# Gated MLP: up projections with tokens on partitions, brought to channels by VectorE and DRAM

## Chip, core and metric

The kernel runs on one core of a Trainium2 chip. The metric is the device time of one execution in microseconds (us), as the median of several runs. A core has TensorE (PE, matrix products into PSUM), VectorE (DVE), ScalarE (ACT), GpSimd (POOL) and SyncE (SP), each with a queue of its own that it works through in order, and 16 DMA engines. PEld is the loading of weights into TensorE. SP's queue issues nearly all DMA transfers.

## What is computed

Two layers of an encoder on 256 tokens of 1024 channels, float32. Each layer has a token mixer (pooling and attention branches) and a gated MLP with a convolution of width 3 over the tokens. The change is in the MLP:

```python
def _conv_ffn(xn, w_up, conv_w, conv_b, w_down):      # xn: 256 x 1024
    a, gval = jnp.split(xn @ w_up, 2, axis=-1)         # w_up: 1024 x 5632
    a = depthwise_conv(a, conv_w, width 3, over tokens) + conv_b
    return (jax.nn.gelu(a) * gval) @ w_down            # w_down: 2816 x 1024
...
h = h + _conv_ffn(_rmsnorm(h, norm2[layer]), ...)
```

## The kernel before

**Numbers.** Float32 products are made of parts: every operand is split into a high part in a shorter format (fp32r) and the rest, and three products (high-high, high-low, low-high) are summed in PSUM. Tokens are in two halves t = 0, 1 (even and odd tokens), 128 each.

**Weights.** The class `Weights` (lines 95 to 223) loads all weights in 1 MB transfers into three buffers `raw` (line 134, on SP's queue) and splits each into two pieces of 128 x 1024: ACT casts the high part `wh` (line 197) and DVE subtracts to get the rest `wl` (line 198). Five pairs of split buffers exist; `W.get` (line 216) asks for pieces three ahead of the one in use. `loads_behind` and `queue_behind` keep named instructions ahead of a load or a split on their queue. The order of the loads and pieces is written out by hand in lines 257 to 299. `cols` takes 256 columns of a weight over all 1024 rows (rows of 1 KB), `rows` takes some rows with 512 or 1024 columns (rows of 2 or 4 KB).

**Order.** A scheduler orders each engine's instructions at build time from the order of the program and from when it thinks that buffers and data are there. On the chip, each engine then keeps that order.

**Two forms of a projection.** In the *channel form* (`proj`, line 528, `two_sums`, line 507) the weight piece is loaded into TensorE and the activations stream past it: 8 matmuls of 512 columns and 8 of 256 give 128 channels on partitions by 256 tokens. `add_up` (line 554) adds the two sums (an ACT copy out of PSUM, then a DVE addition). In the *token form* (`v_sum`, line 638, `by_tokens`, line 649) the activations are loaded into TensorE and 512 columns of the weight stream past: four pieces of 12 matmuls give two PSUM tiles of 128 tokens by 512 channels. `by_tokens` calls `then` after each piece.

**The MLP** has 22 groups of 128 channels (`NF`), f = 0 to 21. The convolution runs over tokens and so needs channels on partitions, and so does the down projection. The first four groups' `a` branch (`ENTRY = 4`) is made in the token form by `begin_mlp` (line 1179) while the norm is still under way, copied out of PSUM (`keep_entry`), transposed on TensorE (`turn_entry`, line 1210, tile `a_turn`) and copied to `a_first`. All other projections are in the channel form. `up(f)` (line 1230) then makes one group: ACT scales (line 1239), two DVE operations add the neighbours (lines 1240, 1243), a tanh form of gelu follows (lines 1252 to 1259), the gate is multiplied in (line 1260), and the product is split into the high part `actq` (line 1265) and the rest `actk` (line 1266). The loop in lines 1284 to 1289 makes two groups and then two steps of the down projection, which runs six groups behind (`LAG = 6`). The down projection is `residual_mm` (line 566): one piece of `w_down`, 12 matmuls into four PSUM tiles, for each group. It holds its last four groups back, so that the four output tiles end one after the other.

**The way through DRAM.** The attention stage has a transposition that the change uses again, `start_turn` (line 1014): DVE transposes blocks of 32 x 32 (line 1019), one transfer writes 512 KB to DRAM (line 1021), and four read it back with the blocks in their places (line 1027). SP issues all five.

Of the kernel before, what the change touches and what calls it, by code (L numbers as in the profile page):

```python
# [10 lines left out]
F32 = mybir.dt.float32  # L11
# [24 lines left out]

WARM = ((P,) * 6, (P // 2,), (P, P // 2))
PAIRS = (2, 4, 0, 1, 3, 5)
LAG = 6
ENTRY = 4  # L40
HALVES = (slice(0, 512), slice(512, D))
SEGMENTS = (HALVES, (slice(0, 512), slice(512, 768), slice(768, D)))

# [183 lines left out]
def encoder(ctx, tc, x, w_in, w_pool, pool_scale, w_a, w_b, w_o, norm1, norm2, w_up, conv_w,  # L227
# [13 lines left out]
    def cols(w, c0):  # L241

        src = w[:, c0 : c0 + 256].rearrange("(k p) c -> p k c", p=P)
        return W.add(
            src, (8, 256), [((lambda t, j=j: t[:, :, j * P : (j + 1) * P]), (8, P)) for j in (0, 1)]
        )

    def rows(w, r0, n=2, c0=0, width=1024, tag=None, pieces=2):

        src = w[r0 : r0 + n * P, c0 : c0 + width].rearrange("(k p) c -> p k c", p=P)  # L250
        h = n // pieces
        return W.add(
            src, (n, width), [((lambda t, j=j: t[:, j * h : (j + 1) * h, :]), (h, width)) for j in range(pieces)],
            tag,
        )

    first_up = []
    for l in range(DEPTH):
        for g in range(NG):
            c0 = C_V + g * 512  # L260
            slots = (("m2", 0, 2), ("m2", 1, 2), ("ybig",), ("at2",)) if g == 0 else ()
            for j in range(2):
                tag = "k1" if l == 0 and g == 1 and j == 0 else None
                W.use(rows(w_in[l], j * 512, 4, c0, 512, tag), slots[2 * j : 2 * j + 2])
        if l == 0:
            W.n_scaled = len(W.pieces)
        for c in range(3, -1, -1):
            W.use(cols(w_in[l], c * 256))
        for n, c in enumerate(PAIRS):
            pool = ([], [])  # L270
            if n == 1:
                pool = W.add(
                    w_pool[l].rearrange("g (k p) c -> p (g k) c", p=P), (8, 256),
                    [((lambda t, j=j: t[:, 4 * j : 4 * j + 4, :]), (4, 256)) for j in range(2)],
                )
                pool = (pool[:1], pool[1:])
            W.use(pool[0] + cols(w_in[l], C_Q + c * 256))
            W.use(pool[1] + cols(w_in[l], C_K + c * 256))
        for w, c0 in ((w_a[l], 0), (w_in[l], C_GP)):
            for c in (c0, c0 + 512):  # L280
                W.use(rows(w, 0, 4, c, 512) + rows(w, 512, 4, c, 512))
        for c in (0, 512):
            W.use(rows(w_in[l], 0, 4, C_GA + c, 512) + rows(w_in[l], 512, 4, C_GA + c, 512))
            W.use(rows(w_b[l], 0, 4, c, 512))
        for c in range(4):
            W.use(rows(w_o[l], c * 256))
        first_up.append((len(W.pieces), len(W.loads)))
        slots = (("v1",), ("ybig",), ("at2",))
        for j in range(2):
            tag = None if j else "k1"  # L290
            W.use(rows(w_up[l], j * 512, 4, 0, 512, tag), slots[2 * j : 2 * j + 2])
        for f in range(0, NF, 2):
            a = cols(w_up[l], f * P) if f >= ENTRY else []
            g = cols(w_up[l], DFF + f * P)
            W.use([a[0], g[0], a[1], g[1]] if a else g)
            if f >= LAG:
                W.use(rows(w_down[l], (f - LAG) * P))
        for f in range(NF - LAG, NF, 2):
            W.use(rows(w_down[l], f * P))


# [248 lines left out]
    def in_order(a):  # L550

        return a.rearrange("p (m t) -> p t m", t=2)

    def add_up(out, sums):

        nc.scalar.copy(out=out, in_=sums[1])
        nc.vector.tensor_add(out=out, in0=sums[0], in1=out)  # L557
# [77 lines left out]
    def v_tile():  # L635
        return acc.tile([P, 512], F32, tag="acc", name="v_ps")
# [26 lines left out]
    def to_chunks(rows, y, z, parts):  # L663
# [12 lines left out]
        made = nc.scalar.copy(out=hi, in_=z), nc.vector.tensor_sub(out=lo, in0=z, in1=hi.bitcast(F32))  # L676
        return turned, there, made

    def two_parts(tag, name):


        return big.tile([P, KD, 2, 2, P], F32R, tag=tag, name=name)
# [174 lines left out]
    for l in range(DEPTH):  # L857
# [154 lines left out]
        turned_p = big.tile([P, 2, 2 * 4, 4, 32], F32, tag="ybig", name="turned_p")  # L1012

        def start_turn(hh):


            y = sm.tile([P, 2, 4, 4, 32], F32, tag="gain", bufs=1, name="turning")
            for t in range(2):
                nc.vector.transpose(out=y[:, t].rearrange("p q c j -> p c q j"), in_=probs[hh, t])
            d = dram.tile([2 * P, 4, P], F32, tag="turning", bufs=2, name="turning")  # L1020
            nc.sync.dma_start(
                out=d.rearrange("(t p) q x -> p t (q x)", t=2),
                in_=y.rearrange("p t q c j -> p t (q c j)"),
            )
            z = turned_p[:, hh % 2]
            for q in range(4):
                there = nc.sync.dma_start(
                    out=z[32 * q : 32 * q + 32].rearrange("p a c j -> p a (c j)"),
                    in_=d[:, q].rearrange("(a i) x -> i a x", i=32),
                )  # L1030

            W.loads_behind[W.n_loaded + 1] = there
            if hh == HPG - 1:
                W.loads_behind[first_up[l][1]] = there

# [164 lines left out]
        acts = {}  # L1200


        a_first = big.tile([P, ENTRY, S], F32, tag="gates", name="a_first")

        def keep_entry(ps):
            r = sm.tile([P, ENTRY * P], F32, tag="p", bufs=3, name="a_rows")
            nc.scalar.copy(out=r, in_=ps)
            return r

        def turn_entry(t, r):  # L1210
            pt = mmp.tile([P, ENTRY, P], F32, tag="mm", name="a_turn")
            for f in range(ENTRY):
                nc.tensor.transpose(pt[:, f, :], r[:, f * P : (f + 1) * P], ident)
            av = a_first.rearrange("p f (m t) -> p f m t", t=2)[:, :, :, t]
            nc.vector.tensor_copy(av, pt)

        held, ps = entry
        first = keep_entry(ps)
        ps = v_tile()
        for n in range(4):  # L1220
            v_sum(ps, x2, 1, n, held[n])
            if n == 1:
                turn_entry(0, first)
        for i, _ in held:
            W.free(i)
        last = keep_entry(ps)
        g_first = [proj(x2)]
        turn_entry(1, last)

        def up(f):  # L1230
            w0, w1, w2, b = (prm[:, l, j * NF + f : j * NF + f + 1] for j in range(4))
            if f < ENTRY:
                a = a_first[:, f, :]
            else:
                a = sm.tile([P, S], F32, tag="u", name="a")
                add_up(in_order(a), [halves(b) for b in proj(x2, 1 + (f < NF - 4))])
            sums = g_first.pop() if f == 0 else proj(x2)
            y = sm.tile([P, S], F32, tag="s", name="y")
            nc.scalar.activation(y, a, AF.Identity, bias=b, scale=w1)  # L1239
            nc.vector.scalar_tensor_tensor(  # L1240
                out=y[:, 1:], in0=a[:, : S - 1], scalar=w0, in1=y[:, 1:], op0=ALU.mult, op1=ALU.add
            )
            nc.vector.scalar_tensor_tensor(  # L1243
                out=y[:, : S - 1], in0=a[:, 1:], scalar=w2, in1=y[:, : S - 1],
                op0=ALU.mult, op1=ALU.add,
            )
            g = sm.tile([P, 2, P], F32, tag="p", bufs=3, name="g")
            add_up(g, [halves(a) for a in sums])

            c = float(np.sqrt(2.0 / np.pi))  # L1250
            y2 = sm.tile([P, S], F32, tag="us", name="y2")
            nc.scalar.activation(y2, y, AF.Square, scale=float(np.sqrt(0.044715)))  # L1252
            nc.vector.scalar_tensor_tensor(
                out=y2, in0=y2, scalar=1.0, in1=y, op0=ALU.add, op1=ALU.mult
            )
            nc.scalar.activation(y2, y2, AF.Tanh, scale=c)
            nc.vector.scalar_tensor_tensor(
                out=y2, in0=y2, scalar=1.0, in1=y, op0=ALU.add, op1=ALU.mult
            )
            nc.vector.scalar_tensor_tensor(  # L1260
                out=g, in0=in_order(y2), scalar=0.5, in1=g, op0=ALU.mult, op1=ALU.mult
            )
            n = f % NH
            ah, al = (x[n >= HPG][:, n - HPG * (n >= HPG)] for x in (acth, actl))
            nc.scalar.copy(out=ah, in_=g)
            nc.vector.tensor_sub(out=al, in0=g, in1=ah.bitcast(F32))
            acts[f] = (ah, al)

        late = {}
        begun = []  # L1270
# [10 lines left out]
            lambda k: acts[k], NF, lambda *a: late["norm"].add(*a),  # L1281
            fill=begin_values if l + 1 < DEPTH else None, whole=(l + 1 == DEPTH),
        )
        for f in range(0, NF, 2):
            up(f)
            up(f + 1)
            if f >= LAG:
                next(down)
                next(down)
        if l + 1 < DEPTH:  # L1290
            x2 = two_parts("x", "x2")
            late["norm"] = Norm(to_channels(x2, mmp, g1))
# [33 lines left out]
```

## Time and profile before

| what | value |
|---|---|
| median of 3 runs | 864.71 us (864.32 to 864.93) |
| profiled execution | 864.36 us, span 862.6 us, granted clock 0.998 |
| busy PE, PEld | 855.9, 738.2 us |
| busy DVE, ACT, POOL | 665.2, 506.6, 32.6 us |
| DMA | 174.23 MB, mean 202 GB/s |
| TensorE in the down projection | 3 groups x184, 69.9 us each |
| weight splitting in all | DVE 331.6 us, ACT 285.4 us |

The busy time of an engine is what its instructions cover; the span runs from the first to the last instruction. A group row names line, engine, operation, written and read tile with shapes and count, then busy time and mean ns of one, then the idle time just before and who ended it. In the timeline, the first two numbers are start and duration in us.

### The profile page before, as it was taken

Reading aid. Unit: us, or ns where it says so; the run is one execution under the profiler, and the core shown is the slowest. Engines: PE = TensorE matmul, PEld = TensorE weight load, DVE = VectorE, ACT = ScalarE, POOL = GpSimd, SP = SyncE. Lnnn points to the kernel's source line nnn. Section 1 sums busy time; section 2 is a strip of 40 time slices with the busy share of each in tenths; the row PEclk is TensorE's granted clock in tenths of the full one; section 3 lists DMA queues with packets and bytes.
Section 4 is the critical chain, followed back from the end, with each engine's and each line's share of the span. In section 5 each row is a group of like instructions: output and inputs, shape, how many; then the busy total and the mean of one; then the engine's idle time right before and its main releaser. Section 6 shows DMA issues by size and latency. Waiting matters only on the chain.

```text
span 862.6 us, 12111 instructions
## 1 busy us (share of the span) xinstructions
PE 855.9 (99%) x4519; PEld 738.2 (86%) x4519; DVE 665.2 (77%) x1070; ACT 506.6 (59%) x831; POOL 32.6 (4%) x98
## 2 busy tenths in 40 slices
PE   9999999999999999999999999999999999999997
PEld 8888888888888888888888888988888888888886
DVE  7998796667769978888855987873776798887874
ACT  7756654455457766666545675543654586666662
POOL 1800000000010000000000000000000000000001
PEclk9999999999999999999999999999999999999999
DMA  9685556766745565565626565648767446556541
GB/s 335 210 253 198 195 169 222 243 229 226 261 164 195 183 211 192 169 229 191 241 98 210 180 202 188 207 171 257 244 236 277 164 150 221 173 189 205 193 147 49
DMA packets 130306, 174.23 MB, mean 202 GB/s; under 512 B 4600, under 2 KB 95424, under 8 KB 130248
## 3 DMA queue, kind: packets, MB, share of 16 engines
q1 hardware_dynamic: 130088, 173.20, 59.6%
q8 instruction: 35, 0.57, 0.3%
q10 hardware_dynamic: 160, 0.27, 0.1%
q14 instruction: 23, 0.19, 0.1%
HBM read 166.09 MB, written 7.36 MB: 201 GB/s over the span
## 4 chain that ended last, share of the span: by engine, by line
PE 99%; DVE 0%; ACT 0%; issue 0%; POOL 0%; POOLq 0%; ACTq 0%
PE proj_ps L520 46%; PE t_ps L644 18%; PE v_ps L644 6%; PE res_ps L562 6%; PE res_ps L563 6%; PE res_ps L564 6%; PE v_ps L849 3%; PE v_ps L756 1%; PE pool_ps L520 1%; PE o_ps L1056 1%; PE s_ps L988 1%; PE s_ps L983 1%; PE o_ps L1052 1%; PE xt_ps L458 1%; PE gain_ps L349 0%; PE xt_ps L704 0%
## 5 line engine op out<-in xcount | busy, mean ns | idle before, releaser
L198 DVE TENSOR_TENSOR wl<-raw,wh 128x1024 fp32r<-128x1024 f32 x274 | 331.6, 1220 | 97.9 <-ACT wh L197 62.2
L197 ACT CAST wh<-raw 128x1024 fp32r<-128x1024 f32 x274 | 285.4, 1050 | 109.4 <-PE t_ps L644 31.6
L520 PE MATMUL proj_ps<-x,wh 128*128 128x512 f32 x1152 | 273.5, 390 | 0.0
L520 PEld LDWEIGHTS proj_ps<-x,wh 128*128 128x128 f32 x1152 | 213.3, 188 | 42.5
L520 PEld LDWEIGHTS proj_ps<-x,wl 128*128 128x128 f32 x1152 | 145.0, 191 | 3.6
L520 PE MATMUL proj_ps<-x,wl 128*128 128x256 f32 x1152 | 147.9, 283 | 0.0
L644 PE MATMUL t_ps<-wh,x 128*128 128x512 f32 x256 | 79.9, 391 | 0.0
L562 PE MATMUL res_ps<-wh,actq 128*128 128x512 f32 (+1 forms) x184 | 69.9, 380 | 0.0
L564 PE MATMUL res_ps<-wh,actk 128*128 128x512 f32 (+1 forms) x184 | 69.9, 380 | 0.0
L563 PE MATMUL res_ps<-wl,actq 128*128 128x512 f32 (+1 forms) x184 | 69.9, 380 | 0.0
L644 PEld LDWEIGHTS t_ps<-wh,x 128*128 128x128 f32 x256 | 47.8, 188 | 9.8
L644 PE MATMUL t_ps<-wl,x 128*128 128x512 f32 x128 | 49.8, 389 | 0.0
L644 PE MATMUL t_ps<-wh,po 128*128 128x512 f32 x128 | 41.4, 395 | 0.0
L563 PEld LDWEIGHTS res_ps<-wl,actq 128*128 128x128 f32 x184 | 34.6, 188 | 6.6
L562 PEld LDWEIGHTS res_ps<-wh,actq 128*128 128x128 f32 x184 | 34.6, 188 | 6.6
L564 PEld LDWEIGHTS res_ps<-wh,actk 128*128 128x128 f32 x184 | 34.6, 188 | 6.6
L1252 ACT ACTIVATE y<-y 128x256 f32<-128x256 f32 x44 | 18.1, 416 | 28.4 <-DVE y L1243 28.3
L431 POOL TENSOR_SCALAR ss<-ss 128x1 f32<-128x1 f32 x8 | 2.2, 275 | 783.2 <-ACT junk L424 783.2
L1239 ACT ACTIVATE y<-a,prm 128x256 f32<-128x256 f32 x36 | 21.6, 600 | 14.7 <-DVE a L557 14.7
L644 PEld LDWEIGHTS t_ps<-wl,x 128*128 128x128 f32 x128 | 24.0, 188 | 5.0
L644 PEld LDWEIGHTS t_ps<-wh,po 128*128 128x128 f32 x128 | 24.0, 188 | 4.9
L424 ACT ACTIVATE junk<-h 128x512 f32<-128x512 f32 (+1 forms) x19 | 10.5, 554 | 29.0 <-DVE h L422 28.8
(206 smaller groups left out, 1170.3 us busy)
## 6 DMA issues: line engine op xcount, KB each, us to landing
raw<-in_w_in_dram SPq DMA_DIRECT2D x58, 1024.0 KB, 5.1
raw<-in_w_up_dram SPq DMA_DIRECT2D x44, 1024.0 KB, 7.1
raw<-in_w_down_dram SPq DMA_DIRECT2D x22, 1024.0 KB, 4.8
raw<-in_w_a_dram SPq DMA_DIRECT2D x8, 1024.0 KB
raw<-in_w_o_dram SPq DMA_DIRECT2D x8, 1024.0 KB
turning<-turning SPq DMA_DIRECT2D x8, 512.0 KB, 3.1
turned_p<-turning SPq DMA_DIRECT2D x32, 128.0 KB, 3.6
raw<-in_w_b_dram SPq DMA_DIRECT2D x4, 1024.0 KB, 4.9
```

The lines of the kernel that those rows point to most:

```text
L197: lambda: nc.scalar.copy(out=h, in_=src),
L198: lambda: nc.vector.tensor_sub(out=l, in0=src, in1=h.bitcast(F32)),
L424: nc.scalar.activation(junk[:, 0 : cc.stop - cc.start], h[:, t, cc], AF.Square, scale=D**-0.5, accum_out=ss[:, n : n + 1],)
L458: nc.tensor.transpose(pt[:, k, :], xn[:, c0 : c0 + P], ident)
L520: nc.tensor.matmul(out, w(k), x, start=(steps is first and k == 0), stop=(steps is last and k == nk - 1), skip_group_check=turns["rest"],)
L562: nc.tensor.matmul(ps, ah, wh, start=first, stop=False, skip_group_check=on)
L563: nc.tensor.matmul(ps, ah, wl, start=False, stop=False, skip_group_check=on)
L564: nc.tensor.matmul(ps, al, wh, start=False, stop=last, skip_group_check=on)
L644: nc.tensor.matmul(ps, x2[:, 2 * n + j, part, t, :], w[:, j, :], start=(n + m == 0), stop=(n == last and m == 5),)
L849: nc.tensor.matmul(ps[t], a[:, k, t, :], w[:, j, :], start=(k + m == 0), stop=(k == KD - 1 and m == 2),)
L1239: nc.scalar.activation(y, a, AF.Identity, bias=b, scale=w1)
L1252: nc.scalar.activation(y2, y, AF.Square, scale=float(np.sqrt(0.044715)))
```

## The change

Both up projections use the token form for f = 0 to 19, in five groups of 512 columns (`NQ = 5`); the channel form stays for f = 20 and 21. Each result (two PSUM tiles of 128 tokens by 512 channels) is brought to channels by `cross`, which is the body of `start_turn` made a function: two DVE transposes of 32 x 32 blocks out of PSUM, a write to DRAM, four reads into `za` (two buffers, `a` branch) or `zg` (one buffer, gate). `activate` (copy out of `za`, convolution, gelu into `soft`) and `times` (`soft` with the gate from `zg`, then the split) take the place of `up`. `then` puts them after the pieces of the next group's projections, with one step of the down projection after each piece of an `a` chunk from the third on. The order in a group n = 2, 3, 4 is: four pieces of `a` with four down steps between, then four pieces of `g`. The transposes on TensorE (`turn_entry`) go. Weights of the up projections are loaded by 512 columns and four blocks of rows, and the loads wait on SP's queue behind the crossing (`loads_behind` in `cross`).

```diff
-LAG = 6
-ENTRY = 4
+NQ = NF // 4
...
-        for f in range(0, NF, 2):
-            a = cols(w_up[l], f * P) if f >= ENTRY else []
-            g = cols(w_up[l], DFF + f * P)
-            W.use([a[0], g[0], a[1], g[1]] if a else g)
-            if f >= LAG:
-                W.use(rows(w_down[l], (f - LAG) * P))
-        for f in range(NF - LAG, NF, 2):
+        def four_up(c0, down=None):
+            for j in range(2):
+                up = rows(w_up[l], j * 512, 4, c0, 512)
+                if down is None:
+                    W.use(up)
+                else:
+                    d = rows(w_down[l], (down + 2 * j) * P)
+                    W.use([up[0], d[0], up[1], d[1]])
+        four_up(DFF)
+        for n in range(1, NQ):
+            four_up(n * 512, 4 * (n - 2) if n > 1 else None)
+            four_up(DFF + n * 512)
+        a, g = cols(w_up[l], 4 * NQ * P), cols(w_up[l], DFF + 4 * NQ * P)
+        for j in range(2):
+            W.use([a[j], g[j]] + rows(w_down[l], (4 * (NQ - 2) + 2 * j) * P))
+        for f in range(4 * (NQ - 1), NF, 2):
             W.use(rows(w_down[l], f * P))
...
+    def cross(rows, y, z, name, but=1):
+        for t in range(2):
+            nc.vector.transpose(out=y[:, t].rearrange("p q c j -> p c q j"), in_=rows[t])
+        d = dram.tile([2 * P, 4, P], F32, tag=name, bufs=2, name=name)
+        nc.sync.dma_start(
+            out=d.rearrange("(t p) q x -> p t (q x)", t=2),
+            in_=y.rearrange("p t q c j -> p t (q c j)"),
+        )
+        for q in range(4):
+            there = nc.sync.dma_start(
+                out=z[32 * q : 32 * q + 32].rearrange("p a c j -> p a (c j)"),
+                in_=d[:, q].rearrange("(a i) x -> i a x", i=32),
+            )
+        W.loads_behind[W.n_loaded + but] = there
+        return there
...
-            if n == 1:
-                turn_entry(0, first)
...
-        last = keep_entry(ps)
-        g_first = [proj(x2)]
-        turn_entry(1, last)
+        to_z((ps0, ps1), za[:, 0])
+        to_z(by_tokens(x2, 4), zg)
...
+        def activate(f):
+            n, i = divmod(f, 4)
+            a = sm.tile([P, S], F32, tag="u", name="a")
+            nc.scalar.copy(
+                out=a.rearrange("p (a j t) -> p t a j", t=2, j=32), in_=of_chunk(za[:, n % 2], i)
+            )
+            soften(convolved(f, a), soft[:, i])
+
+        def times(f):
+            g = sm.tile([P, 2, P], F32, tag="p", bufs=3, name="g")
+            nc.vector.scalar_tensor_tensor(
+                out=g.rearrange("p t (a j) -> p t a j", j=32),
+                in0=soft[:, f % 4].rearrange("p (a j t) -> p t a j", t=2, j=32), scalar=0.5,
+                in1=of_chunk(zg, f % 4), op0=ALU.mult, op1=ALU.mult,
+            )
+            keep_act(f, g)
...
-        for f in range(0, NF, 2):
-            up(f)
-            up(f + 1)
-            if f >= LAG:
-                next(down)
-                next(down)
+        def then(n, branch):
+            pieces = iter(range(4))
+            def work():
+                i = next(pieces)
+                f = 4 * (n - 1)
+                if branch:
+                    if i < 2:
+                        times(f + 2 + i)
+                else:
+                    if n > 1:
+                        next(down)
+                    activate(f + i)
+                    if i > 1:
+                        times(f + i - 2)
+            return work
+        for n in range(1, NQ):
+            to_z(by_tokens(x2, 4, then=then(n, 0)), za[:, n % 2])
+            to_z(by_tokens(x2, 4, then=then(n, 1)), zg)
+        f = 4 * (NQ - 1)
+        for j in range(2):
+            sums = proj(x2, 2), proj(x2)
+            next(down)
+            activate(f + 2 * j)
+            next(down)
+            activate(f + 2 * j + 1)
+            for i in range(2):
+                times(f + 2 * j + i)
+            up(*sums, 4 * NQ + j)
```

## The prediction

> **What bounds the kernel now.** I read the page's busy table and its chain first.
>
> ```profile
> PE 855.9 (99%) x4519; PEld 738.2 (86%) x4519; DVE 665.2 (77%) x1070; ACT 506.6 (59%) x831; POOL 32.6 (4%) x98
> PE 99%; DVE 0%; ACT 0%; issue 0%; POOL 0%; POOLq 0%; ACTq 0%
> ```
>
> TensorE (PE) is busy and is the chain throughout: a stop of it adds to the time one for one, and only work taken from it can shorten the time. Next, whether PE streams the new form faster. Two pieces of the chain in order of time (start us, us):
>
> ```profile
> 144.52 2.77 PE t_ps L644 x12
> 299.18 11.11 PE proj_ps L520 x64
> ```
>
> One weight piece multiplied with tokens on partitions is 12 matmuls and 2.77 us. The channel form takes 11.11 us for four projections, 2.78 each. So the change gives PE nothing for each projection. Then the MLP stage, by windows (us; busy and count of PE, PEld, DVE, ACT, POOL; granted clock, DMA share, GB/s):
>
> ```profile
> 264.00:297.00 33.00, 33.00 (x185) 28.89 (x185) 32.85 (x69) 26.14 (x54) 0.00 (x0) 1.00 0.50 174
> 330.00:363.00 33.00, 33.00 (x178) 28.59 (x177) 26.31 (x45) 21.11 (x37) 0.00 (x0) 1.00 0.58 192
> ```
>
> VectorE (DVE) is full at the MLP's start and has some 7 us free in each 33 us later, ScalarE (ACT) 12, the DMA engines 40%. PE never waits here, so this slack is what the change may use up. The durations, from the groups kept apart by form and from the timeline (start us, us):
>
> ```profile
> L198 DVE TENSOR_TENSOR wl<-raw,wh 128x1024 fp32r<-128x1024 f32 x274 | 331.6, 1220 | 97.9 <-ACT wh L197 62.2 <-PE proj_ps L520 33.7
> L197 ACT CAST wh<-raw 128x1024 fp32r<-128x1024 f32 x274 | 285.4, 1050 | 109.4 <-PE t_ps L644 31.6 <-PE res_ps L564 29.3 <-PE proj_ps L520 24.1
> L1019 DVE STREAM_TRANSPOSE turning<-p 128x512 f32<-128x512 f32 x16 | 10.8, 697 | 0.1
> 254.52 3.90 ACT L197 CAST wh<-raw 128x1024 fp32r<-128x1024 f32 x4
> 258.50 2.35 DVE L198 TENSOR_TENSOR wl<-raw,wh 128x1024 fp32r<-128x1024 f32 x2
> 270.96 0.75 DVE L1260 SCALAR_TENSOR_TENSOR g<-y,g 128x256 f32<-128x256 f32 x2
> 271.74 0.70 ACT L1265 CAST actq<-g 128x256 fp32r<-128x256 f32 x2
> 256.57 0.60 PE L1213 MATMUL a_turn<-ident,a_rows 128*128 128x128 f32 x4
> ```
>
> One is longer than the step to the next: a weight subtraction takes 1.22 us but a pair 2.35 (step 1.13), casts step 0.95, 256-wide operations on DVE 0.33 and on ACT 0.30.
>
> **The change, part by part.** *Taken from PE:* four groups of four `a_turn` transposes; the next matmuls start 0.36 us after a group does, so **-1.4 us**.
>
> *DVE and ACT totals, each layer.* 36 `add_up` pairs go (DVE 0.42, ACT about 0.38: -15.1 and -13.7), as do the `a_first` and `a_rows` copies (-1.4, -1.2). 10 crossings bring 20 transposes at 0.70 (+14.0 on DVE), and 20 copies out of `za` some 0.39 each on ACT (+7.8). DVE gets 2.5 us lighter, ACT 7. A transpose out of PSUM is not in the trace: I take the 0.70 of the row from SBUF, as `add_up` from PSUM (0.42) costs what 256-wide operations from SBUF do. At most I'd let it double (+0.7 where it counts), at least 0.5. None of this is on PE's path by its total.
>
> *DMA.* 20 crossings write 512 KB and read 4 x 128 KB: 21 MB on 174 MB. The rows `turning` (3.1 us to landing) and `turned_p` (3.6), with four issues of 0.44, give about 9 us a crossing. It is wanted more than 11 us after its source, so alone it costs nothing. All of it stands on SP's queue, where weight loads are behind it (a rival below). The `a` and `g` loads now have 2 KB rows, like those of `w_in` (5.1 us to landing, against 7.1 for `w_up` in 1 KB rows).
>
> *What is moved: the order on ACT and DVE.* Each works through its queue in the built order, so I followed the changed program's order with these durations. The steady groups n = 2, 3, 4 go like this. Near the end of an `a` chunk DVE has, in this order, the transpose of t=0, the transpose of t=1, the four products of `times` and their four subtractions, and **only then** the subtraction for the first weight piece of the following `g` chunk. ACT has that piece's cast behind the four copies of `keep_act`. The transpose waits for PE's last matmul of the chunk, so DVE and ACT stand idle ahead of it though the piece's raw data could be there. Let that matmul end at 0. The t=1 transpose starts at 0.05, products from 0.65 (0.33 each; the fourth waits for the first subtraction to free its tile, 2.7), its ACT copy 3.1, the weight cast 3.45 to 4.5, the weight subtraction 4.55 to 5.75. PE has one piece of the down projection (2.77) as cover and can run two matmuls (0.46) from the cast alone. It loses 5.8 - 2.77 - 0.46 = 2.6 us. Three groups, two layers: **+15.4 us**. At n = 1 the four pieces of the `g` chunk stand ahead of the transposes, so nothing is lost.
>
> The second place is the start of the first interleaved `a` chunk (n = 1), with no down piece as cover. DVE has the transposes of the `g` chunk, then the convolution of f = 0, 1 (four 255-wide operations; a dependent one starts 0.52 after its source, others 0.4: to 2.5), then two more, then the weight subtraction. ACT has two squares first, the second from 2.65, then the cast 2.95 to 4.0. Subtraction 4.05 to 5.3; minus 0.46 gives 4.85, twice: **+9.7 us**. The raw data of that weight come behind the first crossing on SP's queue (0.4 issue, 3.1 write, 1.8 for four issues, 0.4 and 5.1 for the load: 10.8 us after its transposes, with the `g` chunk taking 11.1), so before the cast's turn.
>
> The third is the tail. After the last `g` chunk PE runs f = 20 (5.55), and the next down piece's cast and subtraction stand behind the `add_up` of f = 20, whose sums end at 4.57: copy 0.4, square 0.35, cast to 6.35, subtraction to 7.6. Lost 7.6 - 5.55 - 0.46 = 1.6, twice: **+3.2**. From there DVE must do the activations of f = 16 to 21, with 11 weight pieces, in some 36 us; it is 0.3 to 1 us late for the last of them, and in layer 0 its norm products stand behind a sum that waits for PE (1.6). I take 3 and 1: **+4**. The bounds here are 0 and 10.
>
> Sum: -1.4 + 15.4 + 9.7 + 3.2 + 4 = +30.9. The profiled execution took 864.36 (span 862.6), 0.35 below the median of 864.71. So 864.71 + 30.9 = 895.6, rounded to **896**.
>
> With transposes of 1.4 the six g starts and the four others grow by 0.7 each (+7); with 0.5 they shrink by 0.2 (-2). Each hand-over between engines (0.05 in the rows) may cost twice as much: six in a chain, 0.3 for each place, +3.
>
> **Rivals.**
>
> *The clock falls in the stops.* The windows at the end of the span, where PE has ended:
>
> ```profile
> 856.00:857.00 1.00, 0.71 (x6) 0.51 (x5) 0.56 (x2) 0.70 (x3) 0.32 (x2) 1.00 0.72 275
> 858.00:859.00 1.00, 0.00 (x0) 0.00 (x0) 0.49 (x1) 0.70 (x1) 0.27 (x1) 1.00 0.00 0
> 859.00:860.00 1.00, 0.00 (x0) 0.00 (x0) 0.00 (x0) 0.02 (x1) 0.00 (x0) 0.70 0.35 135
> 860.00:861.00 1.00, 0.00 (x0) 0.00 (x0) 0.00 (x0) 0.00 (x0) 0.00 (x0) 0.50 1.01 387
> ```
>
> PE ends at 856.7; the granted clock goes to half at about 859.4, 2.7 us later. At the n = 1 starts PE stands still for 4.0 us on end, at the others 1.7. No row shows how long a fall lasts. If as long as it takes to come, 2.7 us at half speed lose 1.35, or 2.7 in all; if a whole `a` chunk, 11.1 each. I take +5 us: 901. For it: 4.0 is over 2.7. Against: one row, at one phase. The Trainium skill ("TensorE: Matmul & The Clock Gate", Part 1) has a free-running window of about 3.4 us: a full idle one halves the clock, a full busy one restores it. An estimate by that page: 1.7 us for each fall, and a stop of 4.0 would not always hold a full window. The trace's 2.7 us is shorter than that window.
>
> *SP's queue makes it worse.* The `za` crossing of a steady group stands behind a down load that waits for the second `g` piece's subtraction, about 6.9 us after the `a` chunk. It lands at about 17, and PE ends the `g` chunk at 16.4. From then the convolutions and a weight cast take some 6.5 us, PE has 11.1 us of pieces: 4 us are to spare. Two transfers at once at half speed (DMA share goes from 0.58 to some 0.75) would be 8 us late, so 4 lost, six times: 920. Against: the window 220 to 240 us has a share of 0.79 and no stop of PE.
>
> *Not slower.* The mechanism: the following piece is ready in time, because transposes and products need less than the cover. It decides when the first `g` piece is subtracted within 2.77 + 0.46 = 3.2 us of the chunk's end. Then also the n = 1 start would have to be covered. What is left is -1.4: 863.3, no measurable difference. For it speaks that DVE is 20% idle and gets lighter; against it, the order: 4.55 us are in front of that subtraction.
>
> **How the numbers follow.** Forecast (stops as summed, clock held, 888 to 899) 50%; clock 25%; SP's queue 13%; half or fewer of the stops (870 to 887) 6%; not slower 6%. Differences within 0.2% (1.7 us) are what a measurement of this kernel can't tell from none. The not-slower case: 2% faster, 4% same. Slower 94%. The range 880 to 914 takes in forecast, clock and the bounds of the tail, transpose and hand-overs; it leaves out most of SP's queue and the last two cases.
>
> **What would show it.** Right: PE idle of some 2 us in two parts ahead of `t_ps` at the start of the `g` chunks, ended by ACT `wh` and DVE `wl`, about 5 us once in each layer, PE busy time about equal (-1.4), DVE waiting for PE ahead of the `crossing` transposes. Clock rival: windows after the n = 1 starts with a granted clock under 1.00. SP rival: ACT's copies out of `za` waiting for DMA for over 4 us. Wrong: PE idle below 10 us in all, or `wh` waiting for raw data.

## The result and the profile after

The changed kernel takes **910.15 us** (median of 4 runs, 907.14 to 911.6) against 864.53 (4 runs): 1.0523 times, interval 1.0495 to 1.055. The likeliest case of the prediction gave 896, its clock rival 901; 910 lies in the range, 880 to 914, and nearer to its end. The profiled execution took 911.6 us with a span of 909.8, so 47.2 us are to be found against the span of 862.6.

The busy table and the chain of the page after:

```profile
PE 873.1 (96%) x4215; PEld 731.7 (80%) x4215; DVE 662.8 (73%) x1034; ACT 492.7 (54%) x795; POOL 31.3 (3%) x98
PE 87%; DVE 5%; DMA 3%; ACT 2%; issue 1%; SPq 0%; POOL 0%; POOLq 0%; DVEq 0%; ACTq 0%
```

PE is no longer the whole chain: VectorE, ScalarE and DMAs hold 10% of it. PE stands still for 909.8 - 873.1 = 36.7 us, where it was 862.6 - 855.9 = 6.7. Those are 30.0 us. The other 17.2 are in PE's busy time, although its work became less. The MLP windows that were solid before (us; busy of PE, PEld, DVE, ACT, POOL; granted clock, DMA share, GB/s) now read:

```profile
264.00:297.00 33.00, 28.91 (x117) 23.00 (x116) 22.90 (x38) 18.22 (x32) 0.00 (x0) 0.90 0.76 255
330.00:363.00 33.00, 30.35 (x130) 24.50 (x129) 23.08 (x38) 18.77 (x32) 0.00 (x0) 0.97 0.65 223
```

PE has holes, and the clock column is under 1.00. DVE is less busy in these windows (32.85 to 22.90, 26.31 to 23.08) mostly because the same 33 us now hold less of the work: over the whole span it went from 665.2 to 662.8 us, and ACT from 506.6 to 492.7 (2.4 and 13.9 us less, where the prediction has 5 and 14 for the two layers). Now one start of a `g` chunk (n = 2, layer 0), from the timeline (start us, us; in brackets the idle time just before and what ended it):

```profile
317.67 0.39 PE L654 MATMUL t_ps<-wh,x 128*128 128x512 f32 x1
...
320.39 0.39 PE L574 MATMUL res_ps<-wh,actk 128*128 128x512 f32 x1
322.57 0.73 PE L654 MATMUL t_ps<-wh,x 128*128 128x512 f32 x2 [1.79 <-ACT wh L196]
323.83 0.79 PE L654 MATMUL t_ps<-wl,x 128*128 128x512 f32 x1 [0.53 <-DVE wl L197]
...
318.10 0.72 DVE L694 STREAM_TRANSPOSE crossing<-t_ps 128x512 f32<-128x512 f32 x1 [0.34 <-PE t_ps L654]
318.74 1.05 DVE L1285 SCALAR_TENSOR_TENSOR g<-soft,zg 128x256 f32<-128x256 f32 x3
319.71 1.09 DVE L1272 TENSOR_TENSOR actk<-g,actq 128x256 fp32r<-128x256 f32 x3
320.72 0.42 DVE L1285 SCALAR_TENSOR_TENSOR g<-soft,zg 128x256 f32<-128x256 f32 x1
321.61 0.43 DVE L1272 TENSOR_TENSOR actk<-g,actq 128x256 fp32r<-128x256 f32 x1 [0.47 <-ACT actq L1271]
322.55 3.50 DVE L197 TENSOR_TENSOR wl<-raw,wh 128x1024 fp32r<-128x1024 f32 x3 [0.52 <-ACT wh L196]
...
321.48 3.88 ACT L196 CAST wh<-raw 128x1024 fp32r<-128x1024 f32 x4
```

The `a` chunk ends at 318.06. The transpose of t=1 follows at once, then the four products and their subtractions, and the cast of the next weight piece starts 3.4 us after the chunk and ends 4.5 after it; the subtraction follows. PE has one down piece to 320.78 and then waits, first for the cast, then for the subtraction. At n = 1 the convolutions are in front instead:

```profile
274.46 0.80 PE L654 MATMUL t_ps<-wh,x 128*128 128x512 f32 x1 [4.05 <-ACT wh L196]
...
273.38 1.98 ACT L196 CAST wh<-raw 128x1024 fp32r<-128x1024 f32 x2
```

And the clock behind the stop at 320.78, by windows of 1 us:

```profile
322.00:323.00 1.00, 0.43 (x2) 0.30 (x2) 0.48 (x2) 1.00 (x2) 0.00 (x0) 1.00 0.40 152
323.00:324.00 1.00, 0.47 (x3) 0.17 (x2) 1.00 (x2) 1.00 (x2) 0.00 (x0) 0.89 0.00 0
324.00:325.00 1.00, 1.00 (x3) 0.81 (x4) 1.00 (x2) 1.00 (x2) 0.00 (x0) 0.50 0.00 0
```

PE has resumed, and only then does the granted clock fall to half, at about 323.8 to 327.2: the window 323.78 to 327.19 holds 8 matmuls, the equally long one behind it 16. So the busy column looks sound while the work goes at half speed. Over the whole span I added (1 - granted clock) times PE's busy time in windows of half a us. It gives 17.3 us in nine places: 2.5 and 3.1 at the two n = 1 starts, 1.6 to 1.7 after each of the six `g` starts, 1.7 in the tail of layer 1.

| place | predicted, us | trace after, us |
|---|---|---|
| six `g` starts | 15.4 | 15.2 (2.32, 2.65, 2.65 in each layer) |
| two n = 1 starts | 9.7 | 8.1 (4.05 each) |
| first stop of the tail, two | 3.2 | 3.7 (1.29, 2.40) |
| end of the tail | 4 | 3.2, all in layer 0 |
| transposes of PE gone | -1.4 | not measured alone |
| clock | 0; rival +5 | 17.3 |
| sum | 30.9; rival 36 | 47.2: the rows above, with -1.4 for the transposes, make 46.1 |

### The profile page after: what moved, and what is told of

Its sections match the earlier page's. It is cut to its first block, busy times and chain, and to the rows that moved or that the text cites. A ratio compares the mean times of both kernels' runs of the same rounds, so it can differ in the third digit from the quotient of the medians.

```text
span 909.8 us, 11610 instructions
## 1 busy us (share of the span) xinstructions
PE 873.1 (96%) x4215; PEld 731.7 (80%) x4215; DVE 662.8 (73%) x1034; ACT 492.7 (54%) x795; POOL 31.3 (3%) x98
## 4 chain that ended last, share of the span: by engine, by line
PE 87%; DVE 5%; DMA 3%; ACT 2%; issue 1%; SPq 0%; POOL 0%; POOLq 0%; DVEq 0%; ACTq 0%
PE t_ps L654 39%; PE proj_ps L530 21%; PE v_ps L654 6%; PE res_ps L573 4%; PE res_ps L574 4%; PE res_ps L572 4%; PE v_ps L879 2%; DMA raw<-in_w_down_dram 2%; DVE wl L197 2%; ACT wh L196 1%; PE v_ps L786 1%; PE pool_ps L530 1%; DVE g L1285 1%; DVE actk L1272 1%; PE o_ps L1070 1%
## 5 line engine op out<-in xcount | busy, mean ns | idle before, releaser
L654 PE MATMUL t_ps<-wh,x 128*128 128x512 f32 x832 | 273.1, 404 | 20.2 <-ACT wh L196 20.2
L654 PEld LDWEIGHTS t_ps<-wh,x 128*128 128x128 f32 x832 | 161.9, 196 | 57.3 <-ACT wh L196 23.6
L654 PE MATMUL t_ps<-wl,x 128*128 128x512 f32 x416 | 169.2, 407 | 3.2 <-DVE wl L197 3.2
L530 PE MATMUL proj_ps<-x,wh 128*128 128x512 f32 x576 | 136.1, 390 | 0.0
L530 PEld LDWEIGHTS proj_ps<-x,wh 128*128 128x128 f32 x576 | 106.8, 188 | 21.3
L654 PEld LDWEIGHTS t_ps<-wl,x 128*128 128x128 f32 x416 | 82.0, 197 | 24.6 <-DVE wl L197 7.3
L530 PE MATMUL proj_ps<-x,wl 128*128 128x256 f32 x576 | 74.9, 283 | 0.0
L530 PEld LDWEIGHTS proj_ps<-x,wl 128*128 128x128 f32 x576 | 72.8, 191 | 1.9
L694 DVE STREAM_TRANSPOSE crossing<-t_ps 128x512 f32<-128x512 f32 x36 | 25.4, 712 | 46.5 <-PE t_ps L654 46.5
L1278 ACT COPY a<-za 128x256 f32<-128x256 f32 x40 | 15.5, 415 | 41.0 <-DMA za<-crossing 41.0
L1263 ACT ACTIVATE y<-y 128x256 f32<-128x256 f32 x44 | 17.2, 412 | 30.8 <-DVE y L1260 30.7
L1271 ACT CAST actq<-g 128x256 fp32r<-128x256 f32 x44 | 16.4, 406 | 32.1 <-DVE g L1285 28.8
```

The source lines that it names most:

```text
L530: nc.tensor.matmul(out, w(k), x, start=(steps is first and k == 0), stop=(steps is last and k == nk - 1), skip_group_check=turns["rest"],)
L654: nc.tensor.matmul(ps, x2[:, 2 * n + j, part, t, :], w[:, j, :], start=(n + m == 0), stop=(n == last and m == 5),)
L1278: nc.scalar.copy(out=a.rearrange("p (a j t) -> p t a j", t=2, j=32), in_=of_chunk(za[:, n % 2], i))
```

## Experiments

My theory after this: **the order in which VectorE and ScalarE work makes the stops, and each stop makes a fall of the clock.** Rivals: the falls come from something else (the load on the chip); raw weights come late on SP's queue behind the crossings; the crossings' 21 MB have a price of their own.

### The order alone, at the `g` starts

`made` holds the cast and the subtraction of each weight piece, and `W.n_got` is the number of the next piece that TensorE will use.

```diff
+    def behind_split(self, *pieces):
+        with ExitStack() as queued:
+            for i in pieces:
+                for inst in self.made[i]:
+                    queued.enter_context(self.tc.issue_after(inst.ins))
+            yield
...
                     if i > 1:
-                        times(f + i - 2)
+                        with W.behind_split(W.n_got + 6 - 2 * i) if n > 1 else ExitStack():
+                            times(f + i - 2)
...
-            to_z(by_tokens(x2, 4, then=then(n, 0)), za[:, n % 2])
+            ps = by_tokens(x2, 4, then=then(n, 0))
+            with W.behind_split(W.n_got, W.n_got + 1) if n > 1 else ExitStack():
+                to_z(ps, za[:, n % 2])
```

> Only the order on ScalarE and VectorE changes: in the groups n = 2, 3, 4 the cast and the subtraction of the next g chunk's first piece come ahead of the a chunk's transposes, and its second piece ahead of times. Theory (the order makes the six stops, and each stop makes a clock fall): the six stops of 1.8 + 0.5 us and their six falls (1.7 us each, 3.4 us at half speed) go, 6 x 4.0 = 24 us less than the changed kernel's 910, about 886; the windows at 320 to 330 us show a granted clock of 1.00. Rival 1 (the order makes the stops, the falls come from something else, such as the load on the chip): 14 us less, 896, with the clock still falling around 325 us. Rival 2 (raw data come late on SP's queue): the cast waits for its load, and the time stays at 905 to 915.

Measured: **881.11 us** (1.0193, 1.0171 to 1.0215), 29.0 less than the changed kernel. The same start in its timeline:

```profile
316.87 2.00 ACT L196 CAST wh<-raw 128x1024 fp32r<-128x1024 f32 x2 [1.16 <-DMA raw<-in_w_up_dram]
...
317.95 1.23 DVE L197 TENSOR_TENSOR wl<-raw,wh 128x1024 fp32r<-128x1024 f32 x1 [1.78 <-ACT wh L196]
...
320.82 0.62 PE L662 MATMUL t_ps<-wh,x 128*128 128x512 f32 x2
...
322.37 0.71 DVE L702 STREAM_TRANSPOSE crossing<-t_ps 128x512 f32<-128x512 f32 x1
```

The cast starts 1.4 us before the chunk ends (318.27), the subtraction ends 0.9 us after that end, while the down piece runs, and PE goes from the down piece into the `g` chunk without a bracket. The transpose comes 4.1 us after the chunk's end at no cost. All six stops are gone. The span fell by 30.5: 15.5 by the stops' brackets (30.2 to 14.7) and 12.7 by falls (17.3 to 4.6). That is 5 more than I expected; 2.6 of it are falls elsewhere (one of the two after the n = 1 start of layer 1 and the one in the tail of layer 1 went as well), 1.7 the stops, which I had put at 2.3 each. The raw data landed 1.4 us before the chunk's end: at these six places SP's queue was not what the stops waited for.

### And at n = 1

The crossing of the first `g` chunk and the first activation are put behind the first `a` pieces' splits in the same way.

> As e1_g_early, and at n = 1 the crossing of the g chunk and the first convolution of a are behind the first a pieces' cast and subtraction as well. Theory: beside the 24 us of e1 some of the two stops at n = 1 (4.9 us each, with a fall of 2.4 us each) goes: the raw data land some 0.6 us after the chunk's end, so 2 to 3 us of stop are left, and a fall may stay: 4 to 10 us less than e1, 876 to 882. Rival (raw data are what the n = 1 stop waits for): the same as e1 within 2 us, and the cast is ended by the load there.

Measured: **874.44 us** (1.0112, 1.0091 to 1.0134), 6.7 less than the kernel above. Stops of 1.5 + 0.5 us are left at n = 1, ended by a cast that waits for its raw data (ScalarE idle for 12.36 us to 270.65, ended by the load from `in_w_up`). Here SP's queue does bound, as soon as the order doesn't; and these stops made no fall.

### Keep PE going in the stops

`turns["pe"]` is the matmul queued just before; the extra matmuls stand behind it, and their results are overwritten.

```diff
+        if fill:
+            with tc.issue_after(turns["pe"].ins):
+                for _ in range(fill):
+                    nc.tensor.matmul(ps[0], x2[:, 0, 0, 0, :], x2[:, 0], start=True, stop=True)
...
-            to_z(by_tokens(x2, 4, then=then(n, 0)), za[:, n % 2])
-            to_z(by_tokens(x2, 4, then=then(n, 1)), zg)
+            to_z(by_tokens(x2, 4, then=then(n, 0), fill=0 if n > 1 else 17), za[:, n % 2])
+            to_z(by_tokens(x2, 4, then=then(n, 1), fill=8 if n > 1 else 0), zg)
```

> The changed kernel with extra matmuls whose results are overwritten (they stand for no part of the reference): 17 of them ahead of the a chunk of n = 1, 8 ahead of the g chunks of n = 2, 3, 4, so that TensorE goes on during the stops, which stay. Clock theory (an idle TensorE makes the granted clock fall, and the fall costs 15 us in all): the clock stays at 1.00 behind these places, and the time falls by 12 to 15 us, to 895 to 898, although TensorE has more to do. Rival (the fall comes from the load or the schedule, not from TensorE standing still): no gain, 908 to 915, with the falls where they were.

Measured: **900.58 us** (1.0413, 1.0397 to 1.043), 9.6 less. The windows of the n = 1 start, of the changed kernel:

```profile
270.00:275.00 5.00, 0.95 (x3) 0.50 (x2) 3.76 (x8) 2.67 (x5) 0.00 (x0) 0.76 1.05 408
275.00:280.00 5.00, 4.96 (x13) 3.45 (x12) 5.00 (x7) 5.00 (x9) 0.00 (x0) 0.56 0.43 97
```

and of this one:

```profile
270.00:275.00 5.00, 4.54 (x19) 3.11 (x17) 4.21 (x8) 3.13 (x6) 0.00 (x0) 1.00 0.98 383
275.00:280.00 5.00, 4.73 (x21) 3.92 (x22) 5.00 (x9) 5.00 (x9) 0.00 (x0) 1.00 0.48 109
```

PE has more to do and the kernel is faster; behind all eight places the clock stays at 1.00, with ScalarE, VectorE and the DMAs as loaded as before. An idle PE makes the clock fall. The gain is 2.4 us short of the least that I had expected: the first stop of the tail grew to 1.6 + 0.5 in both layers, and falls of 1.7 us follow it at 414 and 858 (the changed kernel had one of these, in layer 1).

### The crossings on another queue

```diff
-            cross(ps, y, z, "crossing", 0)
+            cross(ps, y, z, "crossing", 0, nc.gpsimd)
```

> The crossings' reads and writes are issued from GpSimd's queue in place of SP's, so that no weight load stands behind them. Theory (the order on the engines): the eight stops and their falls stay; only the loads of w_down near the end of each layer come earlier, 0 to 6 us less, 904 to 910. Rival (SP's queue makes the loads late, and that makes the stops): the casts no longer wait, and 20 us or more go, 890 or less.

Measured: **888.33 us** (1.0273, 1.0252 to 1.0294), 21.8 less: the rival's number. But its timeline shows that the experiment was not clean:

```profile
316.31 1.22 DVE L197 TENSOR_TENSOR wl<-raw,wh 128x1024 fp32r<-128x1024 f32 x1
...
318.85 0.71 DVE L694 STREAM_TRANSPOSE crossing<-t_ps 128x512 f32<-128x512 f32 x1
```

The subtractions of the weight pieces now stand ahead of the transposes. The order of VectorE and ScalarE is built from a plan of when things will be ready; with the crossings off SP's queue the plan expects the loads earlier, and places the splits earlier. That it is the plan that did this is my reading of the scheduler; the order itself is in the trace. So moving a DMA rewrote the order on two engines that don't issue it. What the queue itself did can't be read from this run, but the last two kernels below answer it.

### One number

`cross` makes a weight load wait behind its reads: the second load after it where the attention calls it, the first in the MLP. Here it is the second in both.

```diff
-            cross(ps, y, z, "crossing", 0)
+            cross(ps, y, z, "crossing")
```

> The changed kernel with one number different: the weight load that is held behind each crossing's reads is the second one after it, not the first. The order on VectorE that is built from this has the first g piece's subtraction ahead of the a chunk's transposes and of times, without anything said about it. Theory (the order on the engines makes the stops, and it follows from where a load was held on SP's queue): all eight stops and their falls go, as in e5: 864 to 872. Rival (the hold protects the crossings, and without it za and zg land late): stops move to the down pieces behind the activations, 880 or more.

Measured: **870.3 us** (1.007, 1.0056 to 1.0083), 39.9 less from this one number. The eight stops at the chunks are gone without a word about the order of the engines. The order did change; the same start as above reads:

```profile
307.45 1.22 DVE L197 TENSOR_TENSOR wl<-raw,wh 128x1024 fp32r<-128x1024 f32 x1
...
309.79 0.72 DVE L694 STREAM_TRANSPOSE crossing<-t_ps 128x512 f32<-128x512 f32 x1 [0.39 <-PE t_ps L654]
```

The subtraction that the `g` chunk needs first is done ahead of the transposes. The number also lets a load go out earlier on SP's queue, so this run alone does not part order from load; the first experiment does, for the six `g` starts. What is left is mostly the tail, where a new stop came in both layers, and a fall with each:

```profile
415.37 0.50 PE L572 MATMUL res_ps<-wh,actq 128*128 128x512 f32 x1 [3.36 <-ACT actq L1271]
...
413.75 0.48 DVE L1249 SCALAR_TENSOR_TENSOR y<-a,prm,y 128x255 f32<-128x255 f32 x1
414.45 0.76 DVE L1285 SCALAR_TENSOR_TENSOR g<-soft,zg 128x256 f32<-128x256 f32 x2
```

The first products of the last group stand behind the convolution of the next pair, and the down piece waits for them: 3.0 to 3.4 us and 1.7 for the fall, twice.

### All stops, and the price of the traffic

The kernel of the second experiment (n = 1), with the second load held (`but=1`) for the first crossing alone, and in the tail:

```diff
-            up(*sums, 4 * NQ + j)
+            with W.behind_split(W.n_got - 2, W.n_got - 1) if j == 0 else ExitStack():
+                up(*sums, 4 * NQ + j)
```

> e2_all_early, with the load of the first interleaved a chunk's weight put ahead of the first crossing's DMAs on SP's queue, and in the tail the add_up of f = 20 queued behind the split of the next two down pieces. Theory (what e2 has over before is the two n = 1 starts, 2 us each, whose load lands 0.6 us after the chunk's end, and the tail, 1.3 + 2.7 us in each layer): the n = 1 stops and the first tail stop go, 2 x 3.3 = 6.6 us less than e2's 874, about 867 to 869; with the rest of the tail (2.7 us in each layer) left. If nothing but the stops ever cost anything, before's time minus 1.4 plus that rest, 868, is the sum from the other side. Rival (the crossings' 21 MB cost time of their own beside the weight loads): stays at 872 to 875, with casts waiting for raw data in the steady groups.

Measured: **864.14 us** (12 runs; 0.9998 times before, 0.9987 to 1.0009). It is better than I had expected: of the tail's rest, which I put at 2.7 us in each layer, 3.2 are left in layer 0 and 0.3 in layer 1. Two of its MLP windows:

```profile
264.00:297.00 33.00, 33.00 (x147) 27.32 (x146) 26.05 (x44) 19.20 (x35) 0.00 (x0) 1.00 0.85 290
330.00:363.00 33.00, 33.00 (x147) 27.36 (x146) 26.73 (x41) 20.70 (x36) 0.00 (x0) 1.00 0.73 255
```

PE is solid with the crossings on SP's queue and the DMA share at 0.73 to 0.85 (0.50 and 0.58 before). In these windows the 21 MB cost nothing, and the rivals of the queue and of the traffic fall as causes of the stops at the chunks. In this profile PE waits for 3.5 us in all, and yet the time is that of the kernel before: PE's busy time is 851.8 us, 4.1 less than before, where the prediction has 1.4 (the part on PE's work below says why). Of the 3.5 us, 2.48 are here:

```profile
431.29 0.41 PE L476 MATMUL xt_ps<-ident,xn 128*128 128x128 f32 x2 [2.48 <-DVE xn L467]
```

### The norm at the end of layer 0

The last kernel, with the splits of the third and fourth piece of `begin_values` queued behind the residual sum of the first token half (`limit` keeps them from being split ahead of it).

```diff
+            if i == self.limit:
+                break
...
+                if t == 0 and cc.stop == D:
+                    turns["h"] = made
...
+            W.limit = W.n_got + 8
...
+            W.limit = None
+            W.queue_behind((turns["h"],), 2)
             ps, held = v_tile(), [W.get() for _ in range(4)]
```

> e5_but1_tail, with the subtractions of the last two of the following layer's first four weight pieces (ybig, at) queued behind the sum of the first token half's residual, where in e5 they stand ahead of it and TensorE waits 2.48 us for xn. Theory (only stops of TensorE count, and the new form spares it 1.4 us of transposes): the 2.48 us go, 864.1 - 2.5 = 861.6, some 0.3% under the kernel before. Rival (the subtractions come late instead and TensorE waits for at in the value projection): 863 to 866.

Measured: **862.58 us** (12 runs; 0.9976 times before, 0.9967 to 0.9985): 0.24% faster than the kernel before, 1.6 us less than the version above where I expected 2.5. Its profiled execution was the slowest of the twelve (866.91) and still shows a stop of 1.98 us there, with a fall of 1.7 behind it. So that the 2.48 us went is not shown by the profile; the median alone carries the gain.

## Why the prediction was right in the stops and wrong in the clock

**The stops: right in place, cause and size.** 32.3 us were summed for the stops, 30.2 measured. At the `g` start the cast was placed to end 4.5 us after the chunk and ended 4.46 after it; at n = 1 a cast ending at 4.0 gave a stop of 4.05. The working (read VectorE's and ScalarE's queues in the built order, with durations from rows of the profile before, and subtract PE's cover) holds for these places. At n = 1 the subtraction's share (0.8) isn't in the brackets: at half clock the two matmuls on the cast alone last longer and cover it.

**The clock: the step that failed.** The forecast took the clock as held. Its rival named the fall, but let it come "at the n = 1 starts PE stands still for 4.0 us on end, at the others 1.7", that is where a stop is longer than the 2.7 us seen in one row. This term was mis-sized: 5 us where 17.3 came, because all six `g` starts fell too. The row that I used shows when a fall came, not what it needs. What the runs show in its place: a fall comes 2.2 to 4.1 us after PE stopped (at the start above 320.78 to 323.78, with PE going again from 322.57) and lasts 3.4 us, or twice that at n = 1. In the 3.41 us ahead of the fall above (320.36 to 323.78) PE was busy for 1.15. The Trainium skill ("TensorE: Matmul & The Clock Gate", Part 1) has a free-running window of about 3.4 us, and a full idle one halves the clock. The trace agrees with the length of the window (3.41 us) and with its running freely; it does not with the need for a full idle one (1.15 us of work ahead of this fall). All falls of this trace start and end on marks that are whole multiples of 3.413 us apart (the first starts at 272.58, the last at 869.91, 175 windows later), wherever the stops lie.

A stop's length alone doesn't decide: 2.48 us (428.81 to 431.29) made no fall in the kernel with all stops at the chunks mended, 1.98 us (429.85 to 431.83) did in the last one. The marks of each trace say why. The first stop is cut by a mark at 429.87 into two windows, with PE busy for 2.35 and 1.99 us; the second lies in one:

```profile
429.87:433.28 3.41, 1.99 (x17) 2.02 (x18) 2.48 (x6) 1.36 (x5) 1.48 (x4) 1.00 0.64 243
...
429.67:433.09 3.42, 1.45 (x13) 1.29 (x12) 2.67 (x7) 1.98 (x7) 1.56 (x4) 1.00 0.21 78
```

I cut all nine traces into windows at their own marks. Of the 2279 windows at full clock, all 24 in which PE was busy for 1.45 us or less (a few of them behind its last matmul) were followed by half clock, and none in which it was busy for 1.78 us or more; of the six between, at 1.54 to 1.71, three were. So in these runs the clock falls when PE works for less than about half of a window. A window at half clock was followed by another one when PE was busy in it for 2.74 us or less, and by full clock from 3.10 on. (PE's busy time is what the profile models.) It follows that stops of 2.3 to 2.65 us, as at the `g` starts, make a fall only if most of the stop lies in one window. That all six did in the profiled execution is in part luck.

With 30.9 and 17.3, less the 2.1 by which the stops were over-counted, the sum is 46.1 of 47.2 (but see PE's work below). The other executions of the changed kernel show a clock of 0.982 against 0.978, about 0.004 x 909 = 3.6 us or two falls less, and are 0.9 to 4.5 us faster.

**PE's work: a term put at nothing.** The prediction took 2.77 us for a weight piece in the token form from a row of one piece alone, and 2.78 for the channel form, so "the change gives PE nothing for each projection". The chain of the kernel before has a longer row:

```profile
178.10 46.51 PE t_ps L644 x205
```

That is 0.227 us a matmul and 2.72 for the 12 of a piece. For the 72 projections that change their form this is an estimate of 4 us less work, beside the 1.4 of the transposes. The kernel with the stops at the chunks mended bears most of it out (PE's busy time is 4.1 us less, 5.4 by these two). In the changed kernel the sum then leaves some 5 us open and not 1.1; a matmul with no follower is busy for 0.39 us instead of 0.227, which takes up a part at the edges of the stops, but how much was not worked out.

**SP's queue: right that it was no cause at the eight starts** of the changed kernel, where the casts did not wait for raw data. The sign that I had named for this rival, ScalarE's copies out of `za` waiting for DMA for over 4 us, came four times (9.28, 9.29, 4.21 and 6.13 us); at n = 1 PE had a `g` chunk to work on meanwhile. In the tail of layer 1 the queue did have a share, which was not forecast:

```profile
867.39 3.89 ACT L196 CAST wh<-raw 128x1024 fp32r<-128x1024 f32 x4 [0.48 <-DMA raw<-in_w_down_dram]
```

This cast waits for its load, and the first stop there is 1.1 us longer than the one in layer 0 (2.40 against 1.29) and is the one with a fall. What I missed besides is that the queue was the cause of the cause: with the first load held behind each crossing the built order had the splits behind the transposes, with the second one held it had them ahead. It also was next in line: with the order mended, the n = 1 start waits for raw data.

**The tail: right as a sum** (7.2 predicted, 6.9 measured), and that by luck: the first stops were 1.29 and 2.40 where 1.6 was predicted for each, and the end had 3.2 and 0 where 3 and 1 were.

**Not slower: wrong for this order, right as a mechanism.** "The following piece is ready in time" is what the last kernels make true, and the time was 863.3 by that case; 864.14 and 862.58 were measured. That 864.14 came so near is luck as well: 3.5 us of stops were left, and PE's work was lighter by 4.1 us, not 1.4.

## What to carry to other kernels

When a change adds work to engines with time to spare, read what stands **ahead of** the next weight split in each engine's queue at every change of stage, and subtract the cover: over the span VectorE got 2.4 and ScalarE 13.9 us lighter here, and PE stood still for 30 us more. Then price each stop with a fall of the clock: cut the trace into windows at the marks of its falls (3.41 us here), and put up to 1.7 us for each window in which the stop leaves PE busy for less than half the time. Look for the fall behind the stop, where PE's busy column looks full. A load held on one queue, or a DMA moved to another, can rewrite the order of other engines when that order is built from a plan: compare the built orders before crediting the queue.

## What was not expected of the hardware

- Stops of 1.79 + 0.53 and 2.12 + 0.53 us were followed by half clock in six of six places of the profiled execution; with PE kept going by matmuls without use the kernel became 9.6 us faster.
- Over nine traces half clock followed every window of 3.41 us in which PE was busy for 1.45 us or less, and none in which it was busy for 1.78 or more.
- A stop of 4.05 us had a clock of 0.50 for 6.8 us in both layers, two windows in a row, which began 2.2 and 3.4 us into the stop and cost 2.5 and 3.1 us.
- DMA shares of 0.73 to 0.85 over 33 us, 255 to 290 GB/s, went with no wait of PE for data.
- The transposes out of PSUM took 712 ns each in the mean, as those from SBUF did before (697).
